# One diffusion trunk layer on one core: the output projection begun under the last two heads' normalisation, and the SwiGLU transposes moved behind the next group's first product

## The chip, the cores and the metric

The kernel runs on one core of one Trainium2 chip. The metric is device time in microseconds (us) of one execution. An execution under the profiler gives the trace that is read here; its own time stands beside the times of the runs without a profile.

## The reference

One layer of a trunk for 512 latent tokens (`x`, width 2048) and 256 context tokens, all float32. What is computed, in order:

```python
mod = silu(c) @ w_mod + b_mod                    # six rows of 2048: shift, scale, gate, twice
hx  = rms_norm(x, g_pre_mix) * (1 + mod[1]) + mod[0]
u, v, q, k, vv, g, df, db = split(hx @ w_in)     # 1024, 1024, 512, 512, 1024, 1024, 16, 16
a_x = gelu(u) * (w_s @ layer_norm(gelu(v)) + b_s)          # group A, 8 heads, chunks of 128
o   = bidirectional gated linear attention(q, k, vv, df, db; state of the context)   # group B, 4 heads of 256
gla = rms_norm(o per head) * out_g * silu(g)
y   = concat(a_x, gla) @ w_out                   # 2048 x 2048
x   = x + mod[2] * rms_norm(y, g_post_mix)
h2  = rms_norm(x, g_pre_ffn) * (1 + mod[4]) + mod[3]
f   = (silu(h2 @ w1) * (h2 @ w3)) @ w_ffn_out    # SwiGLU, 5632 hidden units
x   = x + mod[5] * rms_norm(f, g_post_ffn)
```

## The kernel before

Every product of two float32 matrices is done as three passes of a 32-bit reduced format (`three`, L298): each operand is split into a high part (a cast on ScalarE, ACT) and a low part (the difference, on VectorE, DVE), and TensorE (PE) multiplies high by high, low by high and high by low. Weights are streamed from HBM by DMAs that SyncE (SP) issues, 512 KB each, into a small ring of tiles, split, and used for 24 matmuls of 128x512. So each pair of contraction steps needs one landed load, one ACT cast of 128x1024, one DVE subtraction of 128x1024, in time.

**Stages around the change.** After the context tokens, four blocks of 512 columns are projected, `vv0`, `vv1`, `g0`, `g1` (PE tiles `vv0a` to `g1a`, 16 steps of 12 matmuls each). Under them the attention of the four heads runs as background work: scores by seven levels (`s`), transposed keys (`ktp`, copied to `ktok`), chunk states (`stp`, `st`), the outputs (`o`, copied to `kq`), the mean of their squares (`ms`), and a normalisation by ACT and DVE that ends in `kq` (L909 to L917). The silu of `g` (`ge`, L957) times `kq` (L965) is split into `yh`, `yl` (L942, `to_parts`): the contraction steps 8 to 15 of the output projection. Steps 0 to 7 come from group A (`reload_a`). Heads 0 and 1 give steps 8 to 11, heads 2 and 3 steps 12 to 15.

Then all background work is drained, the pools of the attention are closed, and the output projection runs in column blocks of 512: `wo0`, `wo1`, `wo2` over all four token tiles, `wo3` over two halves (`project`, L1026). Each block ends in squares for the norm and in a product with the gate row, `yo = y * gate[cg]`. The gate rows are themselves products of `c` with 2048 rows of `w_mod`: 16 loads of 512 KB (`m20w`, then `m21w`), each multiplied and added on DVE into `m20acc` or `m21acc` (L229), and one matmul with ones (`m20ps`, L265), two gate rows of 512 from each. The shift and scale of the second half of the layer are made the same way (`mf0` to `mf12`, with `fmodA`, `fmodB`).

The SwiGLU layer goes through the 5632 hidden units in 11 groups of 512. Each is a Strassen-like scheme of seven half-size products (`p1` to `p7`, tile `f3p` for group 3), whose weight tiles are named by letter (`f3a` to `f3e`, `f3z`, `f3y`), 48 matmuls each. At the end DVE and ACT form the units of 512 tokens (`f3u`, `f3g`), PE transposes them (16 transposes, `f3T`), ACT copies them (`f3t`) and writes them to a buffer in HBM (`g_dr`). The last stage reads that buffer back (`gr`, split into `gh`, `gl`) and multiplies with `w_ffn_out` (`fo`, 40 steps for each of four column blocks, in two chunks of 20; then `fz`). From group 3 on the last gate (`m50` to `m53`, 16 loads of 256 KB each) is made in the background.

**What sets the order.** The code is written out once; background work is a generator that a pump advances by `rate` steps after each contraction step of the foreground (`bg` for attention and transposes, `bgm` for products with `w_mod`). A scheduler then orders each engine's instructions; every engine executes its list in order. A few instructions are pinned to the place at which they were written (`keep_in_program_order`), `m20ps` and `mf12ps` among them. A load waits, on SP's list, until the buffer that it fills is free, and what stands behind it waits too. `load_behind` puts a load of `w_mod` after the weight load issued last.

**Buffers that the change touches.** `st2` holds the weight ring of the projection and the SwiGLU (tag `R`, 4 tiles of 128x1024) and, before, four wide tiles `X`; `fp` holds 29 tiles of 128x512 (`fslot`). `st2` takes the place of `stg`, the ring of the stages before. PSUM has 6 banks for products and 2 for background work.

Of the kernel before, what the change touches and what calls it, by code (L numbers as in the profile page):

```python
# [9 lines left out]
F32 = mybir.dt.float32  # L10
# [8 lines left out]
P = 128  # L19
# [72 lines left out]
def trunk_kernel(ctx, tc, cmat, cmask, x, c, ctxt, c_ctx, w_mod, b_mod, g_pre_mix, g_post_mix, g_pre_ffn,  # L92
# [19 lines left out]
    def slot(name, dt=F32, shape=(P, 512)):  # L112
        return s2.tile(list(shape), dt, tag="s2", bufs=NS, name=name)
# [94 lines left out]

    mod_bg = mod_pool(stg, 3, 1, load_behind)

    def mod_acc(c0, n, parts, cvec, name, tiles, pin=False):
# [42 lines left out]
    def mod_row(base, cb, grow, dst, name, tiles, keep=None, nb=2):  # L254

        n = f"{name}{cb}"
        for acc in mod_acc(base + cb * nb * 512, nb * 512, 1, cx, n, tiles):
            if acc is None:
                yield
        yield  # L260
        for j in range(nb):
            b = cb * nb + j
            gb = slot(n + f"g{j}")
            nc.scalar.dma_start(gb, grow[0:1, b * 512:(b + 1) * 512].to_broadcast([P, 512]))
            ps = bank(n + f"ps{j}", False)  # L265
# [503 lines left out]
    def exp_tables():  # L769
        tc.keep_in_program_order(S.preload_act_table_set("natural_log_exp_and_others"))  # L770
# [175 lines left out]
    def reload_a(k):  # L946
        if 6 <= k < 14:
            t = slot(f"ya{k - 6}")
            nc.sync.dma_start(t, a_dr[k - 6])
            to_parts(t, k - 6)  # L950

    for g in range(2):
        accs = block_ws(w_in[0], OG + g * 512, 4, f"g{g}", reload_a if g == 1 else None)
        evs = []
        for b, ps in enumerate(accs):
            ev = slot(f"ge{g}_{b}")
            S.activation(ev, ps, AF.Silu)  # L957
            evs.append(ev)
        if g == 0:
            exp_tables()  # L960
        while not (head_done[2 * g] and head_done[2 * g + 1]):
            bg.run(1)
        for b, ev in enumerate(evs):
            k = g * 4 + b
            V.tensor_tensor(out=ev, in0=ev, in1=kq[k // 2][:, k % 2, :], op=ALU.mult)  # L965
            to_parts(ev, 8 + k)
    bg.drain()
    bgm.drain()
    gl_ctx.close()
    pp_ctx.close()  # L970


    stg_ctx.close()
    fp = ctx.enter_context(tc.tile_pool(name="fp", bufs=1, reuse_waits="tile"))
    st2 = ctx.enter_context(tc.tile_pool(name="st2", bufs=1, side="right", reuse_waits="tile"))
    g_dr = dr.tile([HID // P, P, 512], F32, name="g_dr")
    gate2_dr = dr.tile([4, 512], F32, name="gate2_dr")

    def fslot(name, dt=F32):
        return fp.tile([P, 512], dt, tag="f", bufs=NF, name=name)  # L980

    def chain_tile(name):
        return st2.tile([P, 1024], F32, tag="X", bufs=4, name=name)

    def raw2(name):
        return st2.tile([P, 1024], F32, tag="R", bufs=4, name=name)
# [21 lines left out]
                pump()  # L1008

    mod_late = (chain_tile, chain_tile, load_behind)  # L1010
    gate = [slot(f"gm{b}") for b in range(4)]

    def mods_out():
        for b in range(2):
# [6 lines left out]
    bgm.add(mods_out())  # L1021
    bgm.rate = 1.5
    oss = cp.tile([P, NT, 4], F32, name="oss")
    yo = [[None] * 4 for _ in range(NT)]

    def project(cg, toks, name):  # L1026
        accs = [bank(f"{name}{t}") for t in toks]
        for k, wp in stream2(w_out[0], cg * 512, 0, KT, name):
            for i, t in enumerate(toks):
                three(accs[i], cut(yT[k], t * P, P), wp, k == 0, k == KT - 1)  # L1030
        for i, t in enumerate(toks):
            S.activation(junk, accs[i], AF.Square, accum_out=oss[:, t, cg:cg + 1])
            yo[t][cg] = fslot(f"yo{t}{cg}")
            V.tensor_tensor(out=yo[t][cg], in0=accs[i], in1=gate[cg], op=ALU.mult)

    def residual(t0):

# [109 lines left out]
    def ffn_top(gi, new):  # L1147

        n = f"f{gi}"
        raw = [None] * NQ  # L1150
        ps = two(n + "p1")
        for q in range(NQ):
            raw[q] = blk(gi, 0, 0, q, new(f"{n}X{q}"))
            product(1, q, ps, parts(raw[q], f"{n}a{q}"), NQ)
            pump()
        u = [fslot(f"{n}u{t}") for t in range(2)]
        for t in range(2):
            S.copy(u[t], ps[t])
        return u, raw

    def ffn_top2(gi, u):

        n = f"f{gi}"
        ps = two(n + "p2")
        for q in range(NQ):
            product(2, q, ps, parts(blk(gi, 1, 0, q, raw2(f"{n}b{q}")), f"{n}b{q}"), NQ)
            pump()
        a1 = [fslot(f"{n}g{t}") for t in range(2)]
        vtt(a1, ps, u, ALU.add)
        for t in range(2):  # L1170
            S.activation(a1[t], a1[t], AF.Silu)
        return a1

    early_u, early_a = [], []

    def ffn_group(gi):
        n = f"f{gi}"
# [23 lines left out]
        for q in range(NQ):  # L1201
# [21 lines left out]
        toks = a1 + u
        for f in range(4):
            ps = bank(f"{n}T{f}", False)
            for t in range(NT):
                T.transpose(ps[:, t * P:(t + 1) * P], toks[t][:, f * P:(f + 1) * P], ident)
            gt = slot(f"{n}t{f}")
            S.copy(gt, ps)
            nc.scalar.dma_start(g_dr[gi * 4 + f], gt)  # L1230
# [17 lines left out]
    def hidden(k0, nk):

        for k in range(k0, k0 + nk, 2):  # L1250
            r = raw2(f"gr{k}")
            nc.sync.dma_start(r.rearrange("p (k c) -> p k c", k=2), g_dr[k:k + 2].rearrange("k p c -> p k c"))
            for j in range(2):
                hi, lo = slot(f"gh{k + j}", F32R), slot(f"gl{k + j}", F32R)
                S.copy(hi, r[:, j * 512:(j + 1) * 512])  # L1255
                V.tensor_tensor(out=lo, in0=r[:, j * 512:(j + 1) * 512], in1=hi.bitcast(F32), op=ALU.subtract)  # L1256
                yield (hi, lo)

    LAST = 4
    wl_ = []  # L1260
# [90 lines left out]
```

## Time and profile before

| | |
|---|---|
| median of 3 runs | 2372.94 us (2368.51 to 2376.49) |
| the profiled execution | 2380.68 us, span of its instructions 2378.9 us |
| PE busy | 2274.8 us, 96% of the span |
| DVE, ACT busy | 1596.6 us (67%), 987.0 us (41%) |
| mean granted TensorE clock | 0.981 |
| chain that ended last | PE 66%, DVE 17%, DMA 12% |

A matmul of 128x512 is recorded with 389 ns, but the next starts 227 ns later: matmuls overlap, so busy time says little, and the count of matmuls in a stretch says what PE could do. Idle time of PE in the middle of a dense stage is time lost, unless another stage makes up for it.

### The profile page before, as it was taken

To read this page: it belongs to the slowest core of one execution; us is meant where nothing else is said; L and a number is where in the kernel's file an instruction comes from. 1 tells how busy PE (TensorE), PEld (TensorE's weight loads), DVE (VectorE), ACT (ScalarE), POOL (GpSimd) and SP (SyncE) were. 2 spreads that over 40 slices of the span, in tenths; PEclk is the share of its full clock that TensorE was granted. 3 is DMA by queue.
4 is the path that set the end of the run, shared out by engine and by line. 5 is a ranking of instruction groups with operands and counts; after the bars stand their busy time and mean duration, and the time that the engine had idled before them with its cause. 6 is when DMAs were issued, how large, how long until landed. Compare 5 with 4: busy or idle time off the path is not lost.

```text
span 2378.9 us, 27845 instructions
## 1 busy us (share of the span) xinstructions
PE 2274.8 (96%) x10386; PEld 1844.1 (78%) x10386; DVE 1596.6 (67%) x2072; ACT 987.0 (41%) x1509; POOL 15.5 (1%) x24
## 2 busy tenths in 40 slices
PE   7999999999996999989899999999999899999998
PEld 2778888788885788767788778887778788888886
DVE  3886577677777745698778878888888632242346
ACT  4443234455574224754343444444344332241232
POOL 0000000000000000000000000000000000000000
PEclk9999999999998999999999999999999999999999
DMA  9967787744434965757667757766676542253344
GB/s 323 338 198 252 244 284 265 242 133 127 139 107 152 312 244 169 229 167 241 203 186 256 227 186 228 248 203 226 203 252 214 187 161 98 98 176 107 105 138 157
DMA packets 252013, 477.30 MB, mean 201 GB/s; under 512 B 21163, under 2 KB 32643, under 8 KB 251877
## 3 DMA queue, kind: packets, MB, share of 16 engines
q1 hardware_dynamic: 241152, 457.78, 58.9%
q10 hardware_dynamic: 10724, 17.74, 2.1%
q8 instruction: 81, 1.33, 0.2%
q14 instruction: 56, 0.45, 0.1%
HBM read 451.33 MB, written 24.13 MB: 200 GB/s over the span
## 4 chain that ended last, share of the span: by engine, by line
PE 66%; DVE 17%; DMA 12%; issue 2%; ACT 2%; SPq 0%; ACTq 0%; DVEq 0%
PE fo L116 18%; PE wo L116 6%; PE f1p L116 3%; PE f4p L116 3%; PE f6p L116 3%; PE f2p L116 2%; PE g0a L116 2%; PE v0a L116 2%; PE u1a L116 2%; PE fz L116 2%; PE vv1a L116 2%; PE cv L116 2%; PE q L116 2%; PE k L116 2%; PE u L116 2%
## 5 line engine op out<-in xcount | busy, mean ns | idle before, releaser
L1256 DVE TENSOR_TENSOR gl<-gr,gh 128x512 fp32r<-128x512 f32 x44 | 28.4, 688 | 32.3 <-ACT gh L1255 32.3
L1255 ACT CAST gh<-gr 128x512 fp32r<-128x512 f32 x44 | 25.1, 618 | 42.1 <-DMA gr<-g_dr 30.8
L993 DVE TENSOR_TENSOR fo_2l<-fo_r,fo_2h 128x1024 fp32r<-128x1024 f32 x8 | 9.8, 1225 | 30.0 <-ACT fo_2h L992 30.0
L832 ACT ACTIVATE lv<-lv 128x1024 f32<-128x1024 f32 x20 | 21.0, 1055 | 19.6 <-DVE lv L831 19.5
L116 PE MATMUL vv0a<-vv_0h,hxh 128*128 128x512 f32 x64 | 28.0, 437 | 0.0
L993 DVE TENSOR_TENSOR fo_0l<-fo_r,fo_0h 128x1024 fp32r<-128x1024 f32 x8 | 9.8, 1224 | 26.3 <-ACT fo_0h L992 26.3
L993 DVE TENSOR_TENSOR fo_18l<-fo_r,fo_18h 128x1024 fp32r<-128x1024 f32 x8 | 9.8, 1226 | 26.2 <-ACT fo_18h L992 26.2
L116 PE MATMUL vv1a<-vv_0h,hxh 128*128 128x512 f32 x64 | 27.0, 422 | 0.0
L1315 ACT ACTIVATE junk<-fc 128x512 bf16<-128x512 f32 x16 | 10.1, 631 | 40.7 <-DVE fc L1314 40.6
L833 DVE TENSOR_TENSOR lv<-lv,kq 128x1024 f32<-128x1024 f32 x20 | 24.4, 1220 | 3.8 <-ACT lv L832 3.8
L116 PE MATMUL g0a<-hxh,g_0h 128*128 128x512 f32 x64 | 26.7, 417 | 0.0
L116 PE MATMUL g1a<-hxh,g_0h 128*128 128x512 f32 x64 | 26.4, 412 | 0.3 <-ACT g_0h L277 0.3
L229 DVE SCALAR_TENSOR_TENSOR m20acc<-m20w,cpair,m20acc 128x1024 f32<-128x1024 f32 x16 | 20.5, 1283 | 8.9 <-DMA m20w<-in_w_mod_dram 8.7
L116 PEld LDWEIGHTS s<-lv 128*128 128x128 f32 x192 | 24.9, 191 | 2.1 <-issue 0.5
L993 DVE TENSOR_TENSOR fo_16l<-fo_r,fo_16h 128x1024 fp32r<-128x1024 f32 x8 | 9.8, 1224 | 24.6 <-ACT fo_16h L992 24.6
L116 PE MATMUL v1a<-v_0h,hxh 128*128 128x512 f32 x64 | 26.3, 410 | 0.0
L116 PE MATMUL vv0a<-vv_0l,hxh 128*128 128x512 f32 x64 | 26.0, 407 | 0.0
L993 DVE TENSOR_TENSOR fo_14l<-fo_r,fo_14h 128x1024 fp32r<-128x1024 f32 x8 | 9.8, 1226 | 23.9 <-ACT fo_14h L992 23.9
L116 PE MATMUL v1a<-v_0l,hxh 128*128 128x512 f32 x64 | 25.9, 404 | 0.0
L116 PE MATMUL vv0a<-vv_0h,hxl 128*128 128x512 f32 x64 | 25.9, 404 | 0.0
L116 PE MATMUL g1a<-hxl,g_0h 128*128 128x512 f32 x64 | 25.8, 403 | 0.0
L116 PE MATMUL v1a<-v_0h,hxl 128*128 128x512 f32 x64 | 25.7, 401 | 0.0
(3876 smaller groups left out, 7949.6 us busy)
## 6 DMA issues: line engine op xcount, KB each, us to landing
fo_r<-in_w_ffn_out_dram SPq DMA_DIRECT2D x80, 512.0 KB
gr<-g_dr SPq DMA_DIRECT2D x22, 512.0 KB
mx4w<-in_w_mod_dram SPq DMA_DIRECT2D x16, 512.0 KB
mx8w<-in_w_mod_dram SPq DMA_DIRECT2D x16, 512.0 KB
mx12w<-in_w_mod_dram SPq DMA_DIRECT2D x16, 512.0 KB
mc4w<-in_w_mod_dram SPq DMA_DIRECT2D x16, 512.0 KB
mc8w<-in_w_mod_dram SPq DMA_DIRECT2D x16, 512.0 KB
mc12w<-in_w_mod_dram SPq DMA_DIRECT2D x16, 512.0 KB
```

The source lines that it names most:

```text
L116: return T.matmul(o, lhsT=l, rhs=r, start=start, stop=stop)
L229: ins = V.scalar_tensor_tensor(out=acc, in0=raw[:, j].rearrange("p i c -> p (i c)"), scalar=cvec[:, k0 + j:k0 + j + 1], in1=acc, op0=ALU.m ...
L832: S.activation(lv, lv, AF.Exp)
L833: V.tensor_tensor(out=lv, in0=lv, in1=kq[h], op=ALU.mult)
L993: V.tensor_tensor(out=wl, in0=src, in1=wh.bitcast(F32), op=ALU.subtract)
L1255: S.copy(hi, r[:, j * 512:(j + 1) * 512])
L1256: V.tensor_tensor(out=lo, in0=r[:, j * 512:(j + 1) * 512], in1=hi.bitcast(F32), op=ALU.subtract)
L1315: S.activation(junk, f, AF.Square, accum_out=fss[:, cg:cg + 1])
```

## The change

The attention's last step (the product with `ge` for heads 2 and 3, and the closing of its pools) moves into the first column block of the output projection, ahead of its contraction step 12 (`attention_end`). Block 0 keeps its result without the gate, and is multiplied with `gate[0]` after block 1. The gate rows are begun at step 12 too; the weight ring is opened before. For that the background rate of `mf*` under `vv` and `g` rises from 0.6 to 0.85, so that it is drained before the projection. The transposes of a group's units are issued after the next group's first product (`turn_hidden`); those of the last group after four steps of the last stage, whose first eight `gh`, `gl` are read back inside group 10. `m50` to `m53` load tiles of 128x512 from `fslot`, one row block at a time, no longer pairs in the weight ring; their rate rises from 0.2 to 0.33 with 16 smaller steps in place of 8. The four wide tiles `X` move from `st2` to `fp`.

```diff
-        per = 1024 // w
+        per = width // w                    # mod_row passes width=nb * 512
...
-    bg.rate, bgm.rate = 2.4, 0.6
+    bg.rate, bgm.rate = 2.4, 0.85
...
+    def gated(g, evs):
+        while not (head_done[2 * g] and head_done[2 * g + 1]):
+            bg.run(1)
+        for b, ev in enumerate(evs):
+            k = g * 4 + b
+            V.tensor_tensor(out=ev, in0=ev, in1=kq[k // 2][:, k % 2, :], op=ALU.mult)
+            to_parts(ev, 8 + k)
...
+        exp_tables()
+        gates.append(evs)
         if g == 0:
-            exp_tables()
-        while not (head_done[2 * g] and head_done[2 * g + 1]):
...
+            gated(0, evs)
-    bg.drain()
     bgm.drain()
-    gl_ctx.close()
-    pp_ctx.close()
     stg_ctx.close()
...
     def chain_tile(name):
-        return st2.tile([P, 1024], F32, tag="X", bufs=4, name=name)
+        return fp.tile([P, 1024], F32, tag="X", bufs=4, name=name)
...
-            yield from mod_row(5 * D, b, g_post_ffn, None, "m5", (raw2, fslot, load_behind), gate2_dr, 1)
+            yield from mod_row(5 * D, b, g_post_ffn, None, "m5", (fslot, fslot, load_behind), gate2_dr, 1)
...
         for k, wp in stream2(w_out[0], cg * 512, 0, KT, name):
+            if before:
+                before(k)
...
+            if before:
+                S.copy(yo[t][cg], accs[i])
+            else:
+                V.tensor_tensor(out=yo[t][cg], in0=accs[i], in1=gate[cg], op=ALU.mult)
+
+    def attention_end(k):
+        nonlocal fp
+        if k == 12:
+            gated(1, gates[1])
+            bg.drain()
+            gl_ctx.close()
+            pp_ctx.close()
+            fp = ctx.enter_context(tc.tile_pool(name="fp", bufs=1, reuse_waits="tile"))
+            bgm.add(mods_out())
+            bgm.rate = 1.5
+            bgm.run(1)
...
-    exp_tables()
-    for cg in range(3):
-        project(cg, range(NT), f"wo{cg}")
+    project(0, range(NT), "wo0", attention_end)
+    project(1, range(NT), "wo1")
+    for t in range(NT):
+        V.tensor_tensor(out=yo[t][0], in0=yo[t][0], in1=gate[0], op=ALU.mult)
+    project(2, range(NT), "wo2")
...
+        if gi == HID // 512 - 1:            # in the last group, after its fifth product
+            for _ in range(8):
+                gT.append(next(src))
...
+        behind.append((gi, a1 + u))
+    def turn_hidden():                      # called after p1, p2 and p5 of a group, and at step 4 of fo
+        while behind:
+            gi, toks = behind.pop()         # the 16 transposes, 4 copies and 4 writes as before
...
-    bgm.rate = 0.2
+    bgm.rate = 0.33
```

The first place is PE's list from the end of `g1a` into `wo0`. `ktp`, `stp`, `o` and `ms` belong to head 3, `wo00h` to the first weight tile of block 0. Before:

```order
L871 MATMUL ktp_1_6389<-mats,kk_6334 128x128 x3
L116 MATMUL stp_1_0_6395<-vv_1_4038,ktok_1_6393 128x256
...
L116 MATMUL o_1_6422<-qt_6404,sini 128x128
L116 MATMUL ms_6438<-sq_6436,mats 128x512 x2
L116 MATMUL mf12ps<-mats,mf12acc 128x1 x8
L116 MATMUL wo_6534<-wo00h,yh_6002 128x512
```

And in the changed kernel:

```order
L871 MATMUL ktp_1_6478<-mats,kk_6387 128x128 x3
L116 MATMUL wo_6438<-wo00h,yh_6049 128x512
...
L116 MATMUL stp_1_0_6484<-vv_1_4038,ktok_1_6482 128x256
...
L116 MATMUL stp_1_1_6487<-vv_1_4036,ktok_1_6482 128x256
L116 MATMUL wo_6438<-wo02h,yh_6126 128x512
...
L116 MATMUL o_1_6541<-qt_6511,sini 128x128
L116 MATMUL wo_6438<-wo04h,yh_6220 128x512
...
L116 MATMUL ms_6557<-sq_6555,mats 128x512 x2
```

48 matmuls of `wo0` now stand between `ktp` and `o`, eight more ahead of `ms`, and 88 between `ms` and step 12, the first that needs heads 2 and 3. `mf12ps` stands ahead of the end of `g1a`.

The second place is SP's list from the last loads of the attention's stage on. `mf12w`, `m20w` are rows of `w_mod`, `wo0r` the projection's weights, `ya` group A's result. Before, and then in the changed kernel:

```order
L203 DMA mf12w_6500<-in_w_mod_dram 128x2x512
L203 DMA mf12w_6503<-in_w_mod_dram 128x2x512
L195 DMA wo0r_6538<-in_w_out_dram 128x2x512
L203 DMA m20w_6559<-in_w_mod_dram 128x1024
L203 DMA m20w_6574<-in_w_mod_dram 128x1024
L203 DMA m20w_6577<-in_w_mod_dram 128x1024
L195 DMA wo0r_6580<-in_w_out_dram 128x2x512
```

```order
L949 DMA ya_6297<-a_dr 128x512
L949 DMA ya_6337<-a_dr 128x512
L195 DMA wo0r_6442<-in_w_out_dram 128x2x512
L195 DMA wo0r_6490<-in_w_out_dram 128x2x512
...
L195 DMA wo1r_6857<-in_w_out_dram 128x2x512
L203 DMA m20w_6727<-in_w_mod_dram 128x1024
L203 DMA m20w_6742<-in_w_mod_dram 128x1024
```

All eight loads of `wo0` and the first two of `wo1` now stand ahead of the first load for the gates.

The third place is PE's list at the end of group 10 (`f10p` its last product, `fo` the last stage, `m53ps` the last gate's matmul). Before, and then in the changed kernel:

```order
L116 MATMUL f10p_14701<-f10y3h,S7l_8512 128x512
L1227 MATMUL f10T_14864<-mats,f10g_14437 128x128
...
L1227 MATMUL f10T_14888<-mats,f10u_14355 128x128
L116 MATMUL m53ps_14898<-m53acc,mats 128x512
L116 MATMUL fo_14902<-fo_0h,gh_14914 128x512
```

```order
L116 MATMUL f10p_14753<-f10y3h,S7l_8516 128x512
L116 MATMUL m53ps_14942<-m53acc,mats 128x512
L116 MATMUL fo_14946<-fo_0h,gh_14714 128x512
...
L116 MATMUL fo_14949<-fo_2h,gl_14729 128x512
L1276 MATMUL f10T_15016<-mats,f10g_14452 128x128
```

48 matmuls of `fo` stand ahead of the transposes. On SP seven of the sixteen `m53w` loads now stand between the last load of group 10 and the first of `fo`, where before none did, and four `gr` loads stand ahead of the last eight weight loads of group 10 (`f10z`, `f10y`).

## Rows read from the trace of the kernel before

**Rows 1.** Windows of 10 us at the projection's start: us, busy time (instructions), clock, DMA, GB/s.
```profile
762.00:772.00 10.00, 2.22 (x7) 1.86 (x8) 5.41 (x10) 3.55 (x4) 0.95 (x1) 0.50 0.51 174
772.00:782.00 10.00, 8.87 (x32) 6.68 (x31) 8.23 (x8) 1.04 (x1) 0.00 (x0) 0.75 0.97 344
```

**Rows 2.** Waits of PE, 700 to 840 us: total, times, longest.
```profile
PE mf12ps L116 <- issue: 7.9, 1, 7.9
PE wo L116 <- ACT wo00h L992: 7.8, 1, 7.8
PE stp L116 <- ACT ktok L873: 2.4, 2, 1.8
PE ms L116 <- ACT sq L903: 1.8, 1, 1.8
```

**Rows 3.** Waits of SP's queue, 700 to 780 us.
```profile
SPq L195 <- DVE kq L917: 12.9, 1, 12.9
```

**Rows 4.** Timeline of PE: start us, us, what (two places).
```profile
732.25 0.49 PE L871 MATMUL ktp<-mats,kk 128*128 128x128 f32 x3
...
826.64 0.39 PE L116 MATMUL wo<-wo10h,yh 128*128 128x512 f32 x1
```

**Rows 5.** Chain that ended last, PE's pieces: start us, us, what.
```profile
695.76 0.43 PE stp L116 x2
...
702.53 2.68 PE o L116 x24
...
714.94 1.72 PE ms L116 x4
...
814.16 0.86 PE m20ps L116 x2
...
1890.28 435.49 PE fo L116 x1920
```

**Rows 6.** Timeline of ACT, 737 to 770 us.
```profile
737.79 0.48 ACT L873 COPY ktok<-ktp 128x384 f32<-128x384 f32 x1 [0.36 <-PE ktp L871]
...
754.02 1.28 ACT L911 ACT_TABLE_LOAD   x1
...
765.67 0.62 ACT L942 CAST yh<-ge 128x512 fp32r<-128x512 f32 x1 [9.07 <-DVE ge L965]
...
769.47 1.04 ACT L992 CAST wo00h<-wo0r 128x1024 fp32r<-128x1024 f32 x1 [1.28 <-DMA wo0r<-in_w_out_dram]
```

**Rows 7.** Gate tiles: ns min/median/max of one, first and last start us.
```profile
L229 DVE SCALAR_TENSOR_TENSOR m20acc<-m20w,cpair,m20acc x16: 1278/1284/1286, 771.3 to 805.4; 128x1024 f32<-128x1024 f32 x16
...
L229 DVE SCALAR_TENSOR_TENSOR m21acc<-m21w,cpair,m21acc x16: 1274/1283/1289, 809.1 to 848.2; 128x1024 f32<-128x1024 f32 x16
```

**Rows 8.** Window of the gates' loads, columns as in rows 1.
```profile
770.00:850.00 80.00, 74.68 (x299) 58.09 (x300) 60.28 (x52) 16.81 (x22) 0.96 (x1) 0.94 0.91 309
```

**Rows 9.** Window of the stages vv0 to g1.
```profile
465.00:732.00 267.00, 265.98 (x1426) 225.41 (x1425) 203.32 (x338) 155.49 (x323) 1.91 (x2) 0.99 0.40 129
```

**Rows 10.** Waits of PE in the SwiGLU groups, 1080 to 1860 us.
```profile
PE f2p L116 <- DVE f2c0l L993: 5.7, 1, 5.7
PE f0T L1227 <- DVE f0g L1141: 1.9, 1, 1.9
PE f5p L116 <- ACT f5d0h L992: 1.3, 1, 1.3
...
PE f4T L1227 <- ACT f4t L1229: 0.2, 1, 0.2
PE f6p L116 <- DVE f6a2l L993: 0.2, 1, 0.2
```

**Rows 11.** Timeline of DVE and PE at the end of group 10.
```profile
1855.64 1.30 DVE L1141 TENSOR_TENSOR f10u<-f10p,f10u 128x512 f32<-128x512 f32 x2
...
1877.36 0.39 PE L116 MATMUL f10p<-f10y3h,S7l 128*128 128x512 f32 x1
```

**Rows 12.** Wait of PE, 1860 to 1900 us.
```profile
PE f10T L1227 <- DVE f10g L1141: 5.5, 1, 5.5
```

More of the change, by code (lines that the diff above doesn't have):

```diff
@@ L209, in trunk_kernel, with mod_acc @@
     mod_bg = mod_pool(stg, 3, 1, load_behind)
-    def mod_acc(c0, n, parts, cvec, name, tiles, pin=False):
+    def mod_acc(c0, n, parts, cvec, name, tiles, pin=False, width=1024):
         w = parts * n
@@ L256, in mod_row @@
         n = f"{name}{cb}"
-        for acc in mod_acc(base + cb * nb * 512, nb * 512, 1, cx, n, tiles):
+        for acc in mod_acc(base + cb * nb * 512, nb * 512, 1, cx, n, tiles, width=nb * 512):
             if acc is None:
@@ L950, in reload_a @@
             to_parts(t, k - 6)
+    def gated(g, evs):
[5 more added lines that the diff above has]
+            to_parts(ev, 8 + k)
+    gates = []
     for g in range(2):
@@ L958, in trunk_kernel @@
             evs.append(ev)
+        exp_tables()
+        gates.append(evs)
         if g == 0:
-            exp_tables()
-        while not (head_done[2 * g] and head_done[2 * g + 1]):
[L962 to L966, printed above, removed]
-    bg.drain()
+            gated(0, evs)
     bgm.drain()
-    gl_ctx.close()
-    pp_ctx.close()
     stg_ctx.close()
-    fp = ctx.enter_context(tc.tile_pool(name="fp", bufs=1, reuse_waits="tile"))
     st2 = ctx.enter_context(tc.tile_pool(name="st2", bufs=1, side="right", reuse_waits="tile"))
@@ L1010, in trunk_kernel @@
     mod_late = (chain_tile, chain_tile, load_behind)
-    gate = [slot(f"gm{b}") for b in range(4)]
+    gate = [None] * 4
     def mods_out():
+        for b in range(4):
+            gate[b] = slot(f"gm{b}")
         for b in range(2):
@@ L1018, in gate_ffn, with project @@
         for b in range(4):
-            yield from mod_row(5 * D, b, g_post_ffn, None, "m5", (raw2, fslot, load_behind), gate2_dr, 1)
-    bgm.add(mods_out())
-    bgm.rate = 1.5
+            yield from mod_row(5 * D, b, g_post_ffn, None, "m5", (fslot, fslot, load_behind), gate2_dr, 1)
     oss = cp.tile([P, NT, 4], F32, name="oss")
     yo = [[None] * 4 for _ in range(NT)]
-    def project(cg, toks, name):
+    def project(cg, toks, name, before=None):
         accs = [bank(f"{name}{t}") for t in toks]
         for k, wp in stream2(w_out[0], cg * 512, 0, KT, name):
+            if before:
+                before(k)
             for i, t in enumerate(toks):
@@ L1033, in project @@
             yo[t][cg] = fslot(f"yo{t}{cg}")
-            V.tensor_tensor(out=yo[t][cg], in0=accs[i], in1=gate[cg], op=ALU.mult)
+            if before:
[13 more added lines that the diff above has]
+            bgm.run(1)
     def residual(t0):
@@ L1158, in ffn_top @@
             S.copy(u[t], ps[t])
+        turn_hidden()
         return u, raw
@@ L1171, in ffn_top2, with hidden @@
             S.activation(a1[t], a1[t], AF.Silu)
+        turn_hidden()
         return a1
+    def hidden(k0, nk):
+        for k in range(k0, k0 + nk, 2):
+            r = raw2(f"gr{k}")
+            nc.sync.dma_start(r.rearrange("p (k c) -> p k c", k=2), g_dr[k:k + 2].rearrange("k p c -> p k c"))
+            for j in range(2):
+                hi, lo = slot(f"gh{k + j}", F32R), slot(f"gl{k + j}", F32R)
+                S.copy(hi, r[:, j * 512:(j + 1) * 512])
+                V.tensor_tensor(out=lo, in0=r[:, j * 512:(j + 1) * 512], in1=hi.bitcast(F32), op=ALU.subtract)
+                yield (hi, lo)
     early_u, early_a = [], []
+    gT, src = [], hidden(0, 20)
     def ffn_group(gi):
@@ L1190, in ffn_group @@
             pump()
+        turn_hidden()
         p6 = two(n + "p6")
@@ L1222, in ffn_group @@
         vtt(u, u, p7, ALU.mult)
[L1223 to L1230, printed above, removed]
+        behind.append((gi, a1 + u))
+    behind = []
+    def turn_hidden():
+        while behind:
+            gi, toks = behind.pop()
+            n = f"f{gi}"
+            for f in range(4):
+                ps = bank(f"{n}T{f}", False)
+                for t in range(NT):
+                    T.transpose(ps[:, t * P:(t + 1) * P], toks[t][:, f * P:(f + 1) * P], ident)
+                gt = slot(f"{n}t{f}")
+                S.copy(gt, ps)
+                nc.scalar.dma_start(g_dr[gi * 4 + f], gt)
     bg.rate = 1.0
@@ L1246, in trunk_kernel @@
     facc = [[None] * 4 for _ in range(NT)]
[L1248 to L1257, printed above, removed]
     LAST = 4
@@ L1276, in trunk_kernel @@
     for ci, (k1, nk) in enumerate(((0, 20), (20, 20))):
-        gT = []
-        src = hidden(k1, nk)
+        if ci:
+            gT, src = [], hidden(k1, nk)
         for cg in range(4):
@@ L1284, in trunk_kernel @@
             for k, wp in stream2(w_ffn_out[0], cg * 512, k1, nk, f"fo{ci}{cg}_"):
-                if cg == 0:
+                if len(gT) <= k:
                     gT.append(next(src))
+                if k == 4:
+                    turn_hidden()
                 for t in range(NT):
```

1 line of the change is left out of this document (added).

## The prediction

> **What bounds the kernel now.** I read the windows of the span first: PE is busy 96% of it, so time can only be won where PE stands or runs at the lower clock. Then the chain that ended last: its largest piece is `fo`, 1920 matmuls in 435.49 us, or 0.2268 us for each [rows 5]. That is PE's pace with nothing missing, and I count every stretch against it. The stretch that falls short most lies between the projections and the output projection. In the timeline head 3's `ktp` begins at 732.25 and the first matmul of `wo1` at 826.64 [rows 4]: 94.4 us. The work in it is 192 matmuls of `wo0` (43.5), two heads' `o` (2 x 2.68), `ms` (1.7), six `stp` at half of 0.43 (1.3) [rows 5], six `ktp` at a third of 0.49 (1.0) [rows 4], 16 `mf12ps` at a twenty-fourth of 2.68 each (1.8) and two pairs of `m20ps` (2 x 0.86) [rows 5]: 56.4 us. So 38.0 us are lost there. The waits of PE name half of it: 7.9 ahead of `mf12ps`, 7.8 on `wo00h`, 2.4 on `ktok`, 1.8 on `ms` [rows 2]. The rest is a low clock, 0.50 and then 0.75 of full speed in the two windows where `wo0` starts [rows 1], dependent single matmuls of `stp`, and weights of `wo0` that come late. The last follows from SP's queue: the first load of `wo0` stood 12.9 us behind `kq` [rows 3], and when it went out, the gates' loads stood between those of `wo0`, with the DMA engines busy 0.97 of the time [rows 1].
>
> In the SwiGLU groups PE waits little: five waits at transposes, from 1.9 to 0.2 (3.8 together), and nine for weights from group 3 on, from 1.3 to 0.2 (6.9 together), beside one of 5.7 at `f2c0l` [rows 10]. At the end of group 10 it waits 5.5 ahead of the transposes [rows 12]. The last product begins its last matmul at 1877.36 [rows 11], `fo` starts at 1890.28 [rows 5]: 12.9 us.
>
> **The change part by part.**
>
> *The attention's end.* PE gets 48 matmuls of `wo0` (10.9 us) between `ktp` and `o`, eight more ahead of `ms`, and 88 (20.0 us) between `ms` and step 12. The normalisation that these 88 cover ran in the trace from `kq`'s squares to the cast of `yh`, with two ACT table loads of 1.28 in it [rows 6]. The wait of 7.9 was one for the mean and the last `mf12acc`; `mf12` is now done earlier, and 20 us cover the normalisation. What is left is the front: ACT has two evictions of `ge`, then `ktok` 0.48, a table load 1.28, `yh` 0.62 and `wo00h` 1.04 [rows 6] before the first matmul of `wo0`, some of it under `ktp` and `stp`. I take 4 us for that, and 2 us for `o`, `ms` and single late casts: 6 lost in place of 38.0, a gain of 32. If the 20 us didn't hide the normalisation and the clock stayed low, only the two waits at the front that loads caused (7.8) would go; if PE ran without a hole, 36. Bounds 8 and 36.
>
> *Transposes behind the next product.* The 16 transposes are work all the same; what goes are the waits of 3.8 [rows 10]. PE's list was interleaved before too: the transposes stood among the next group's matmuls, only earlier. I take 3, bounds 0 and 3.8.
>
> *`m5` out of the weight ring.* With it goes a competitor for the ring's four tiles from group 3 on, the cause I see for the nine waits of 6.9 in all [rows 10]. But the smaller loads wait for a free tile of `fslot`, and while one waits, the weight loads behind it on SP's list wait too. Of the 29 tiles I count 16 for the two sums, 6 for `u`, `g` and the products, 4 held units and one accumulator, so two stay free. I take half, 3.5; bounds -3 (the waits grow by half) and 6.9. The wait of 5.7 at `f2c0l` stands before `m5` begins and stays.
>
> *From group 10 into `fo`.* Of the 12.9 us, 16 transposes at 2.68/24 (1.8) and one `m53ps` (0.9, as `m20ps`) remain work [rows 5], so 10 can be won. Against it: four `gr` loads now stand ahead of the `f10z`, `f10y` weights on SP's list. Where `f10u`'s end at 1855.64 [rows 11] comes ahead of the split of `f10z` on DVE, as it now stands, I cost about 4 us at `p5`; and the third and fourth bank of `fo` come free behind the same chain of DVE, 1 us. I take 5; bounds 0 and 10.
>
> *`mf12` drained earlier.* Some 12 additions of 1.28 (as the like gate rows, [rows 7]) move under `vv0` to `g1`, where DVE is busy 203.32 of 267 us [rows 9]: 219 of 267, 0.82 of the time. PE has 0.99 of full clock there and no room, so each late weight counts. I take a cost of 2; bounds 0 and 5.
>
> *The gates.* `m20ps` and `m21ps` are pinned in PE's list, at step 8 of `wo1` and step 4 of `wo2`. The gates' first load now stands behind ten loads of `wo`. With four ring tiles and 24 matmuls (5.44 us) for each load it can go out about 31 us after the end of `g1a`. Before, the additions took from 771.3 to 849.5 [rows 7], 78 us; with 6 for the first load to land, the second gate is ready 115 us after `g1a`. PE arrives at `m21ps` after 432 matmuls (98.0), the other work (some 11) and the front of 4: at 113. I take a cost of 2; bounds 0 and 11 (first load two ring tiles later, 2 x 5.44). `m20ps` has about 7 us of slack by the same count. While `m21ps` waits, the rest of `wo2` is queued behind it.
>
> The gain is 32 + 3 + 3.5 + 5 - 2 - 2 = 39.5 us. The profiled execution took 2380.7 (its span 2378.9 and 1.8 around it), which gives 2341. It lies 7.7 us above the median of the runs, 2372.9; taken from that, 39.5 gives 2333.
>
> **Rivals.** *B: half is given back at the gates.* Over the 80 us of the gates' loads the DMA engines were busy 0.91 of the time, moving 309 GB/s [rows 8]. 16 MB and a bit more of gate rows must still pass, now under PE at full pace, which draws `wo`'s weights faster. Then `m21ps` waits the 11, weights come some 5 later, and the 5 of the end are not won: a gain of 39.5 - 9 - 5 - 5 = 20, 2353. For it: the share; against: the loads begin some 30 us earlier relative to the matmuls that need them. [...]
>
> *C: all terms at their better ends*: 35 + 4 + 7 + 10 and no costs, 56, hence 2317. For it: PE's lists have no other hole; against: six terms must all hold.
>
> *E: the change doesn't do what it says*: the loads of `wo0` wait after all for a tile that the attention holds, as the 12.9 of [rows 3], and PE still stands until the normalisation is over. Only the 8 of the lower bound remain: 2365. Against it: SP's list has `wo0`'s loads right behind `ya`.
>
> *D, slower: SP's list blocks at `m5`'s tiles.* 64 loads of 256 KB need an `fslot` tile each with two free. If one is not free until the units of a group are written out, SP holds the weights behind it. From 0.62 us for each (39.5 / 64) the gain is gone, and at 1.28, the duration of one addition that a load would wait for [rows 7], the time is 2333 + 82 = 2415. For it: only two tiles to spare. Against it: an addition frees a tile at once, and eight loads fall on a group, which lasts some 71 us (780 us of [rows 10] in 11 groups).
>
> **How the numbers follow.** Forecast 2333, chance 0.62; B 0.15, C 0.12, E 0.06, D 0.05. The forecast's own terms with errors of half their bounds give 2322 to 2343. For eight in ten I take in C's half and B: 2314 to 2356. A measurement of this kernel can tell about 0.3%, 7 us, from no change. Faster by more: the forecast, B, C and most of E, less what I don't see, 0.90; within it 0.05 (the rest of E, D at small price); slower 0.05 (D).
>
> **What would show it.** Right: PE's waits on `wo00h` and ahead of `mf12ps` are gone; the clock is at 1.0 of full from `g1` into `wo1`; the first matmul of `wo1` comes about 62 us after head 3's `ktp`; the wait ahead of `f10T` is gone and `fo` begins right behind `f10p` and `m53ps`. The price shows as waits at `m20ps`, `m21ps` (step of the gates), at `f10z` (step of the end), and in SP's queue at `m5w`. Wrong it is if PE stands at step 12 of `wo0` (the normalisation not covered), if `m21ps` waits over 11, or if the waits for weights in groups 3 to 10 exceed 10 together.

## The result and the profile after

The changed kernel took 2347.27 us (median of four runs, 2346.42 to 2349.05), where the kernel before took 2372.8: a ratio of 0.9894 (95% interval 0.9876 to 0.9912), 25.5 us less. Run again beside the experiments it took 2345.56, ratio 0.9875 (0.9861 to 0.9888), 29.6 us less. The forecast was 2333. The direction was right and the time is inside the range, but a quarter to a third of the gain that was forecast (39.5) did not come, and the parts came out differently from their terms.

| | before | after |
|---|---|---|
| profiled execution, span | 2380.68, 2378.9 us | 2349.05, 2347.2 us |
| PE busy | 2274.8 us (96%) | 2262.3 us (96%) |
| DVE, ACT busy | 1596.6, 987.0 us | 1593.5, 982.2 us |
| mean granted clock | 0.981 | 0.990 |
| chain that ended last | PE 66%, DVE 17%, DMA 12% | PE 64%, DMA 15%, DVE 15% |

Where the time went is read from the starts of the first matmuls of each stage, by which a trace is cut into stretches; the last one ends at the start of the last matmul. All the kernels run here are in one table (us, one execution in each row; the time ahead of `vv0` also varies, by up to 9 us, before anything changed is reached, and is left out):

| kernel | vv0 to g0 | g1, attention, wo0 | wo1, wo2 | wo3 | groups 0-2 | groups 3-9 | group 10 to end |
|---|---|---|---|---|---|---|---|
| before | 211.8 | 163.5 | 89.0 | 49.0 | 269.6 | 563.9 | 570.7 |
| before2 (again) | 209.0 | 158.3 | 89.6 | 48.1 | 267.4 | 563.4 | 570.3 |
| after | 213.7 | 130.0 | 102.2 | 49.0 | 261.8 | 563.7 | 567.2 |
| after2 (again) | 212.2 | 127.7 | 102.2 | 48.1 | 263.8 | 563.5 | 566.7 |
| att | 211.8 | 127.7 | 102.5 | 48.0 | 269.1 | 570.8 | 572.8 |
| turn | 210.1 | 159.7 | 89.9 | 48.9 | 261.0 | 563.5 | 566.0 |
| m5 | 210.5 | 161.7 | 88.8 | 48.6 | 268.0 | 566.7 | 572.4 |
| nom5 | 212.9 | 127.7 | 100.8 | 48.7 | 262.3 | 563.6 | 567.0 |
| nopre | 213.4 | 129.7 | 101.6 | 48.6 | 263.2 | 564.0 | 565.9 |
| late | 213.2 | 127.6 | 101.2 | 48.1 | 262.0 | 566.3 | 574.0 |
| slow | 212.3 | 127.1 | 102.7 | 48.3 | 262.7 | 564.1 | 568.1 |
| evict | 214.4 | 127.3 | 92.9 | 48.6 | 263.0 | 564.2 | 566.6 |
| pre4 | 211.8 | 128.1 | 92.9 | 48.2 | 264.7 | 564.0 | 562.8 |
| comb | 214.2 | 127.6 | 93.8 | 48.2 | 265.2 | 565.2 | 566.2 |

By the means of the two executions of each kernel the stretches change by +2.6, -32.0, +12.9, 0, -5.7, 0 and -3.6, together -25.8: the difference that the runs show. The single execution that the prediction was made from stood 11.5 us above the second one over these stretches, 5.2 of it at the attention, so it was a long example of its kernel, and the comparison of the first two traces (31.6 us) overstates the gain.

The hole is closed. PE's timeline, as in [rows 4], shows head 3's `ktp`, the first matmul of `wo0` and that of `wo1` (start us, us, what):

```profile
737.20 0.49 PE L871 MATMUL ktp<-mats,kk 128*128 128x128 f32 x3
...
741.30 0.96 PE L116 MATMUL wo<-wo00h,yh 128*128 128x512 f32 x3 [0.47 <-ACT wo00h L995]
...
793.73 0.39 PE L116 MATMUL wo<-wo10h,yh 128*128 128x512 f32 x1
```

From `ktp` to `wo1` 56.5 us pass where it was 94.4. Of the work counted there, `mf12ps` (1.8) and `m20ps` (1.7) have moved out, so 52.9 are work and 3.6 are lost, in place of 38.0. In the second execution of each kernel it is 56.5 in place of 89.2. The windows of 10 us, columns as in [rows 1], show the granted clock that goes with it: the first two lie at `wo0`'s start and stand at full speed, the third, in `wo2`, at 0.74. The last is the like of [rows 8]:

```profile
741.00:751.00 10.00, 9.70 (x43) 7.92 (x43) 6.62 (x8) 4.09 (x6) 0.00 (x0) 1.00 0.53 183
751.00:761.00 10.00, 10.00 (x69) 8.93 (x67) 1.71 (x2) 3.28 (x4) 0.00 (x0) 1.00 0.30 104
...
842.70:852.70 10.00, 3.25 (x9) 2.35 (x8) 8.36 (x10) 0.76 (x1) 0.00 (x0) 0.74 0.93 318
790.00:870.00 80.00, 71.38 (x296) 56.50 (x295) 55.05 (x51) 19.41 (x32) 0.96 (x1) 0.96 0.85 287
```

PE's waits from 690 to 870 us, in place of [rows 2] (waits of 7.9, 7.8, 2.4 and 1.8), have a new line at their head (the four longest):

```profile
PE wo L116 <- DVE yo L1042: 6.7, 1, 6.7
PE wo L116 <- DVE wo114l L996: 1.5, 1, 1.5
PE stp L116 <- ACT ktok L873: 0.7, 1, 0.7
PE wo L116 <- ACT wo00h L995: 0.5, 1, 0.5
```

L1042 is the eviction of a finished accumulator with its gate row, here of `wo1`'s. It frees a PSUM bank: of the six banks `wo1` holds four, so the third accumulator of `wo2` waits for it. PE's timeline has the place:

```profile
842.63 0.39 PE L116 MATMUL wo<-wo20h,yl 128*128 128x512 f32 x1
849.77 0.79 PE L116 MATMUL wo<-wo20h,yh 128*128 128x512 f32 x1 [6.75 <-DVE yo L1042]
850.36 0.63 PE L116 MATMUL wo<-wo20l,yh 128*128 128x512 f32 x1
...
854.48 0.39 PE L116 MATMUL wo<-wo20h,yl 128*128 128x512 f32 x1
```

`wo1`'s last matmul began at 841.27, and its gate row had been written by 828.3. What held the eviction is DVE's own list, in its timeline (in brackets the idle time before, and what ended it):

```profile
842.49 1.28 DVE L229 SCALAR_TENSOR_TENSOR m21acc<-m21w,cpair,m21acc 128x1024 f32<-128x1024 f32 x1 [0.33 <-DVE m21acc L229]
845.32 1.28 DVE L229 SCALAR_TENSOR_TENSOR m21acc<-m21w,cpair,m21acc 128x1024 f32<-128x1024 f32 x1 [1.55 <-DMA m21w<-in_w_mod_dram]
846.52 1.22 DVE L996 TENSOR_TENSOR wo22l<-wo2r,wo22h 128x1024 fp32r<-128x1024 f32 x1
847.83 1.28 DVE L229 SCALAR_TENSOR_TENSOR m21acc<-m21w,cpair,m21acc 128x1024 f32<-128x1024 f32 x1
849.03 2.47 DVE L1042 TENSOR_TENSOR yo<-wo,gm 128x512 f32<-128x512 f32 x4
```

The evictions stand behind additions for the other gate, which wait for their loads, and these take 5.6 us each while the DMA engines are 0.93 busy. The chain that ended last has one of these loads as a piece of its own; the addition at 845.32 follows it:

```profile
839.63 5.60 DMA m21w<-in_w_mod_dram
```

After the stop the matmuls follow each other 0.43 us apart from 850.36 to 854.20, then 0.23 again: 2 us more. The granted clock is 0.50 from 850 to 854 and 1.00 from 854.4 to 860. The Trainium skill (TensorE: Matmul & The Clock Gate, "Wait — 56ns, not 53.3ns?") gives 426.7 ns between matmuls of 512 columns at 1.2 GHz and 215.7 at 2.4; the trace agrees with the first, and shows 226.8 for the second [rows 5], which is what the sums here use.

### The profile page after: what moved, and what is told of

Read it like the earlier page. It is cut to its first block, busy times and chain, and to the rows that moved or that the text cites. A ratio compares the mean times of both kernels' runs of the same rounds, so it can differ in the third digit from the quotient of the medians.

```text
span 2347.2 us, 27855 instructions
## 1 busy us (share of the span) xinstructions
PE 2262.3 (96%) x10386; PEld 1836.9 (78%) x10386; DVE 1593.5 (68%) x2072; ACT 982.2 (42%) x1509; POOL 15.5 (1%) x24
## 4 chain that ended last, share of the span: by engine, by line
PE 64%; DMA 15%; DVE 15%; issue 3%; ACT 2%; SPq 0%; DVEq 0%; ACTq 0%
PE fo L116 19%; PE wo L116 4%; PE f1p L116 3%; PE f9p L116 3%; PE f2p L116 3%; PE vv1a L116 2%; PE u1a L116 2%; PE fz L116 2%; PE cv L116 2%; PE g1a L116 2%; PE f7p L116 2%; PE q L116 2%; PE vv0a L116 2%; PE u L116 2%; PE g0a L116 2%
## 5 line engine op out<-in xcount | busy, mean ns | idle before, releaser
L229 DVE SCALAR_TENSOR_TENSOR m20acc<-m20w,cpair,m20acc 128x1024 f32<-128x1024 f32 x16 | 20.5, 1284 | 12.6 <-DMA m20w<-in_w_mod_dram 12.4
L996 DVE TENSOR_TENSOR fo_8l<-fo_r,fo_8h 128x1024 fp32r<-128x1024 f32 x8 | 9.8, 1226 | 26.2 <-ACT fo_8h L995 26.2
L996 DVE TENSOR_TENSOR fo_0l<-fo_r,fo_0h 128x1024 fp32r<-128x1024 f32 x8 | 9.8, 1223 | 25.5 <-ACT fo_0h L995 25.5
L996 DVE TENSOR_TENSOR fo_10l<-fo_r,fo_10h 128x1024 fp32r<-128x1024 f32 x8 | 9.8, 1224 | 24.1 <-ACT fo_10h L995 24.1
L229 DVE SCALAR_TENSOR_TENSOR m21acc<-m21w,cpair,m21acc 128x1024 f32<-128x1024 f32 x16 | 20.5, 1282 | 7.9 <-DMA m21w<-in_w_mod_dram 7.3
L996 DVE TENSOR_TENSOR fo_12l<-fo_r,fo_12h 128x1024 fp32r<-128x1024 f32 x8 | 9.8, 1226 | 23.5 <-ACT fo_12h L995 23.5
L116 PE MATMUL g0a<-hxh,g_0l 128*128 128x512 f32 x64 | 25.7, 402 | 0.0
```

What stands on the lines that cost most here:

```text
L116: return T.matmul(o, lhsT=l, rhs=r, start=start, stop=stop)
L996: V.tensor_tensor(out=wl, in0=src, in1=wh.bitcast(F32), op=ALU.subtract)
```

## The experiments

Each kernel ran beside the kernel before, and ratios are to that kernel, so that kernels of different series are compared by ratio or by the stretches above.

**One part at a time: att, turn, m5, and the kernel before once more.** The whole diff is split in three; the wide tiles `X` in the other pool and the rate of 0.85 belong to att.

```diff
 # att = changed kernel with these undone:
-        turn_hidden()          # after p1, p2, p5, and at step 4 of fo
+        turn_hidden()          # at the end of its own group
-                gT.append(next(src))   # eight, inside group 10
-  "m5", (fslot, fslot, load_behind) ... bgm.rate = 0.33
+  "m5", (raw2, fslot, load_behind) ... bgm.rate = 0.2
 # turn = kernel before, with only the first two of these changes
 # m5   = kernel before, with only the third
```

> The attention part alone on the kernel before: projection begun early, its first block kept without the gate, X tiles in the other pool, rate 0.85 under vv and g; transposes, m5 and the reading back of group 10 as before. Theory (the two traces: start of wo3 19.7 us earlier, of which 13 were lost again at the gates): about 20 us of the change's 25.5 are this part, ratio 0.992 (2353), with the same wait of about 7 us for the evictions of wo1. Rival (terms of the prediction): 32 - 2 - 2 = 28 us, 0.988, and the other parts lose a little.

> The transposes behind the next product and the reading back inside group 10 alone on the kernel before; attention and m5 as before. Theory (traces): nothing in groups 3 to 9, 4 us at the f2c0l wait and in groups 0 to 2, 3 to 6 at the end: 5 to 9 us, ratio 0.997. Rival (the prediction's terms): 3 + 5 = 8 us, half of it in groups 3 to 9. Second rival: the wait at f2c0l stays 5.7 and only the end is won: 4 us, 0.998.

> m5's loads alone as 128x512 tiles of fslot at rate 0.33, on the kernel before. Prediction's term: waits for weights in groups 3 to 10 fall from 6.9 to about half, 3.5 us, ratio 0.9985. Rival (trace of the changed kernel: as many waits, at other places): 0 within 2 us, 1.000. Seven m53w loads then stand ahead of fo's: if these delay fo, slower by 1 to 4 us.

> The kernel before, unchanged, profiled once more: whether the 7.7 us by which its profile lay above its median belong to one execution. If so its time is within 4 us of 2373, and the waits of 7.9 and 7.8 us ahead of mf12ps and wo0 are the same while others are shorter. Rival: profiling always costs this kernel 7 us, 2380.

Measured: att 2364.63 us, ratio 0.9957 (0.9941 to 0.9974), 10 us faster; turn 2363.01, 0.9950 (0.9931 to 0.9969), 12 us faster; m5 2378.88, 1.0016 (1.0000 to 1.0032), no gain and up to 8 us lost; before2 2367.35 in its one execution. So profiling does not cost this kernel 7 us; two executions of one kernel differ by that much. The waits of 7.9 and 7.8 were there again (6.8 and 7.9).

att fell short of both of its expectations and turn went beyond its own. m5 gained nothing, as its rivals had it, and not the 3.5 of the prediction. In the table the transposes' part gains 7.5 us in groups 0 to 2 and 4.5 behind group 9, nothing between; the first is the wait at `f2c0l`, which the prediction had left standing. DVE's timeline of the kernel before, and then of the changed one, shows why it went:

```profile
1165.97 2.36 DVE L1188 TENSOR_TENSOR f2X<-f2X,f2c 128x1024 f32<-128x1024 f32 x2
1169.20 1.23 DVE L1188 TENSOR_TENSOR f2X<-f2X,f2c 128x1024 f32<-128x1024 f32 x1 [0.88 <-DMA f2c<-in_w_ffn_in_dram]
1174.01 1.23 DVE L1188 TENSOR_TENSOR f2X<-f2X,f2c 128x1024 f32<-128x1024 f32 x1 [3.58 <-DMA f2c<-in_w_ffn_in_dram]
1175.15 1.28 DVE L1141 TENSOR_TENSOR f2g<-f2p,f2u 128x512 f32<-128x512 f32 x2
1176.35 1.22 DVE L993 TENSOR_TENSOR f2c0l<-f2X,f2c0h 128x1024 fp32r<-128x1024 f32 x1
```

```profile
1145.03 2.35 DVE L1225 TENSOR_TENSOR f2X<-f2X,f2c 128x1024 f32<-128x1024 f32 x2
1150.00 1.23 DVE L1225 TENSOR_TENSOR f2X<-f2X,f2c 128x1024 f32<-128x1024 f32 x1 [2.63 <-DMA f2c<-in_w_ffn_in_dram]
1151.15 1.22 DVE L996 TENSOR_TENSOR f2c0l<-f2X,f2c0h 128x1024 fp32r<-128x1024 f32 x1
```

The split that PE needs, `f2c0l`, depends on the first of four additions. Before, it stood in DVE's list behind all four and two products, and the last addition waited 3.58 us for its load. With the transposes moved the scheduler puts it behind three. Both att (wait 5.5) and m5 (5.2) keep the old order, turn and the whole change (1.9, 1.8) have the new one: the part is shown, though it is the order on DVE that changed and not a wait of the transposes.

att won 33 us at the attention (its stretch against the mean of 160.9), lost 13 in `wo1` and `wo2`, and then 7 more in groups 3 to 9, where it changes no line, only the pool of the wide tiles `X`. Its longest waits from there to the end of group 10, beside `f10T`'s, stand at places where the kernel before has none:

```profile
PE f7p L116 <- DVE f7e0l L996: 2.7, 1, 2.7
PE f7T L1271 <- DVE f7g L1164: 2.4, 1, 2.4
PE f9p L116 <- DVE f9c1l L996: 1.8, 1, 1.8
PE f10p L116 <- DVE f10c1l L996: 1.5, 1, 1.5
```

On DVE's list `f7e0l` stands there behind the group's additions of `f7u` and `f7w`, before it stood ahead of them. The three ratios multiplied give 0.9923, the whole 0.9875 to 0.9894, so 7 to 11 us of the whole's gain belong to no part alone. By the table they lie in groups 3 to 9, where att loses 7.1, m5 3.0 and the whole nothing.

**The wait at `wo2`: evict and slow.** There are two theories of the 13 us. The prediction's step said that `m21ps` stands too early in PE's list. The trace says that the evictions stand too late in DVE's.

```diff
 # evict                                        # slow
-            if before:                          yield from mod_row(2 * D, b, ...)
+            if cg < 2:                         +bgm.rate = 1.0
                 S.copy(yo[t][cg], accs[i])
 ...
     project(2, range(NT), "wo2")
+    for t in range(NT):
+        V.tensor_tensor(out=yo[t][1], in0=yo[t][1], in1=gate[1], op=ALU.mult)
```

> The changed kernel, but wo1's four accumulators are copied out by ACT as wo0's are, and multiplied with gate[1] after wo2; loads, rates and pins unchanged. Theory: the 6.9 us at wo2's third bank come from DVE's list, where the evictions stand behind gate additions that wait for their loads; without it PE does not stop, the clock does not fall (2 us more), and m21ps finds its sum nearly done: 6 to 9 us faster than the changed kernel, 2339. Rival (the prediction's step): the data of m21 are what is late, and the wait moves to m21ps or to wo2's weights: 0 to 3 us, 2345 to 2347.

> The changed kernel with the rate of the gates' background work 1.0 in place of 1.5 from the second gate row pair on: on PE's list m21ps moves from step 4 of wo2 to step 10, while SP's and DVE's lists keep the loads and additions where they are. The prediction priced the gates by m21ps standing too early: then the loss in wo2 falls by 7 or more. Theory now: the stop is at the evictions of wo1 behind the additions on DVE, so the wait of about 7 stays and wo2 lasts the same 54 us.

Measured: evict 2343.24 us, ratio 0.9847 (0.9829 to 0.9865); `wo1` and `wo2` take 92.9 us in place of 102.2. (By ratio alone evict and after2, below, still touch: 0.9865 and 0.9861.) All that PE waits for from 780 to 900 us is this:

```profile
PE wo L116 <- DVE wo114l L996: 0.5, 1, 0.5
PE wo L116 <- DVE wo14l L996: 0.2, 1, 0.2
PE wo L116 <- DVE wo22l L996: 0.2, 1, 0.2
```

The additions still wait for their loads, as this one of DVE's timeline:

```profile
848.16 1.28 DVE L229 SCALAR_TENSOR_TENSOR m21acc<-m21w,cpair,m21acc 128x1024 f32<-128x1024 f32 x1 [1.85 <-DMA m21w<-in_w_mod_dram]
```

`m21ps` stands where it stood on PE, and PE does not wait at it. In slow (2344.13 in one execution) `m21ps` came 39 us after `wo2`'s first matmul in place of 20, and the wait did not go, it grew to

```profile
PE wo L116 <- DVE yo L1043: 8.7, 1, 8.7
```

with 102.7 us for `wo1` and `wo2`. So the place of `m21ps` was not the cause, and the evictions' place on DVE was. What remains in evict over the kernel before, 92.9 against 89.3, is `m20ps` (1.7, moved here) and some 2 us of small gaps.

**m5 taken back: nom5.**

```diff
-  "m5", (fslot, fslot, load_behind) ... bgm.rate = 0.33
+  "m5", (raw2, fslot, load_behind) ... bgm.rate = 0.2
```

> The changed kernel with m5's loads back in the weight ring at rate 0.2: attention and transposes only. Theory A (the parts add): m5 alone cost 4 us on the kernel before, so without it 2343. Theory B (m5's loads matter only with the new timing: the attention part alone lost about 7 us in groups 7 to 9 with the ring shared): 2350 to 2354. Theory C (which waits the order of the groups happens to have): within 2 us of 2347.

Measured: 2345.25 us, ratio 0.9855 (0.9836 to 0.9874), against 0.9894 and 0.9875 with m5 moved. Groups 3 to 9 take 563.6, as with it (563.7, 563.5) and before (563.9, 563.4). Theory B of this expectation falls: with the transposes moved too, the ring shared with `m5` costs nothing there. Between A and C the intervals don't decide; that the move gains nothing by itself is shown by the run m5, whose interval begins at 1.0000. nom5 has `X` in the same pool as att and differs from it in the transposes and the reading back alone, and loses nothing there, so the pool alone does not cost att its 7 us.

**The reading back in group 10: nopre, late, pre4.** The changed kernel waits in group 10 and starts `fo` without a gap. Its waits from 1060 to 1900 us, in place of [rows 10, 12], and PE's timeline at `fo`'s start, in place of [rows 11]:

```profile
PE f10p L116 <- ACT f10z0h L995: 2.3, 1, 2.3
PE f2p L116 <- DVE f2c0l L996: 1.8, 1, 1.8
PE f10p L116 <- DVE f10y0l L996: 1.7, 1, 1.7
PE f5p L116 <- DVE f5c3l L996: 1.2, 1, 1.2
...
PE f1T L1276 <- ACT f1t L1278: 0.2, 1, 0.2
```

```profile
1855.92 0.40 PE L116 MATMUL f10p<-f10y3h,S7l 128*128 128x512 f32 x1
1856.16 1.02 PE L116 MATMUL m53ps<-m53acc,mats 128*128 128x512 f32 x2
1856.62 0.80 PE L116 MATMUL fo<-fo_0h,gh 128*128 128x512 f32 x1
```

```diff
         vtt(u, p4, u, ALU.add)
-        if gi == HID // 512 - 1:
-            for _ in range(8):                 # nopre: none at all
-                gT.append(next(src))           # pre4 (on evict): range(4)
 ...
             product(7, q, p7, parts(y, f"{n}y{q}"), NQ)
+            if gi == HID // 512 - 1 and q >= 2:     # late
+                for _ in range(4):
+                    gT.append(next(src))
```

> The changed kernel without the eight gh, gl read back inside group 10; fo reads them back itself as before. Theory (prediction's cost of 4 us at p5, trace 2.5 at f10z0 and 1.9 at f10y0): group 10 is 4 to 6 us shorter; fo then waits for its first gl behind DVE's chain of group 10, and if that costs as much as before (about 5) the time is the same, 2347. Rival: fo's first gl comes before the chain and nothing is lost: 2342.

> The changed kernel with the eight gh, gl read back four at the third and four at the fourth step of group 10's last loop, so that two gr loads stand behind two pairs of f10z, f10y on SP's list and the rest behind three. Theory: the waits at f10z0 and f10y0 (4.4) go and fo still starts without a wait: 4 to 5 us faster than the changed kernel, 2342. Rival: the waits move to f10z3 and f10y3, 2346 to 2347.

> The changed kernel with wo1 copied out by ACT (as in the run evict) and four gh, gl read back inside group 10 in place of eight. Theory: evict's 8 us, and group 10 and fo's first block together 2 to 4 us shorter than with eight (f10z0's split now stands ahead of half of the gl on DVE): 10 to 12 us faster than the changed kernel. Rival: the same 6 us are lost wherever the reading back stands, since f10's chain on DVE must end before the third bank of fo is free: 8 us, as evict.

Measured: nopre 2350.53 us, ratio 0.9884 (0.9865 to 0.9903), the same as the changed kernel; late 2356.18, 0.9907 (0.9890 to 0.9923), slower than after2's 0.9875, though the interval of the first series reaches into it; pre4 2336.5, 0.9843 (0.9823 to 0.9862). PE's longest waits from 1740 to 1900 us show where the time goes in nopre, then late, then pre4:

```profile
PE fo L116 <- ACT gh L1206: 2.1, 1, 2.1
PE fo L116 <- DVE f10w L1164: 1.3, 1, 1.3
```

```profile
PE fo L116 <- ACT fo_0h L995: 5.8, 1, 5.8
PE fo L116 <- DVE fo_0l L996: 1.7, 1, 1.7
```

```profile
PE f10p L116 <- DVE f10b2l L996: 0.6, 1, 0.6
PE f10p L116 <- DVE f10y2l L996: 0.5, 1, 0.5
PE fo L116 <- DVE f10w L1166: 0.3, 1, 0.3
```

What the reading back saves `fo` it takes from group 10, so eight gain nothing (567.0 with them, 565.9 without). Late only pushes `fo`'s own weights back. With four, in pre4, `f10z0l` stands on DVE ahead of half of the `gl`, and neither side waits long: the last stretch takes 562.8, in evict, with eight, 566.6. That is one execution of each, and the ratios don't show it: pre4 has 0.9843, evict 0.9847.

**What beats both: after2, comb.** comb is pre4 with m5 back in the ring.

```diff
 # pre4, and
-  "m5", (fslot, fslot, load_behind) ... bgm.rate = 0.33
+  "m5", (raw2, fslot, load_behind) ... bgm.rate = 0.2
```

> The changed kernel, unchanged, on the same chip as the next ones, so that these are compared with it and not with times of another chip. Theory: ratio to the kernel before as in the result, 0.989; the wait of about 7 us at wo2's third bank and those at f10z0 and f10y0 are there again. Rival: the ratio depends on the chip and comes out under 0.986, as the two variants that were faster.

> As pre4, and m5's loads back in the weight ring at rate 0.2. Theory: m5's move is worth nothing within 2 us, so the time is that of pre4; no m53w load then stands ahead of fo's loads, which may give 1 to 2 us. Rival: m5's move costs 4 us or more (as on the kernel before), and this is the fastest, 4 to 9 us ahead of pre4.

Measured in one series: after2 2345.56 us, ratio 0.9875 (0.9861 to 0.9888), comb 2335.0, 0.9829 (0.9816 to 0.9843), pre4 0.9843. comb is 0.5% ahead of the changed kernel, its interval clear of that of after2; pre4 overlaps by a hair. comb and pre4 can't be told apart: by their intervals m5's place in the ring is worth between 9 us won and 2 lost. Nor does comb repeat pre4's last stretch. It takes 566.2 in comb's trace, which is the slowest of its five executions (2341.76), and PE waits in group 10 again, at another place:

```profile
PE f10p L116 <- DVE f10y1l L996: 2.1, 1, 2.1
```

So a gain of four read back over eight is not shown; what both share with evict is `wo1` and `wo2` in 93 to 94 us.

## Why the prediction was right in sign and too large

The steps as the prediction put them, with the mean of two traces of each kernel:

- **The attention's end, 32: 31.8.** From `ktp` to `wo1` 91.8 us became 56.5, of which 3.5 is work that moved out (forecast: about 62, with that work still counted). The waits on `wo00h` and ahead of `mf12ps` went (0.5 is left), the clock stayed at full, nothing waits at step 12. But the normalisation was not only covered, it also became shorter: from `kq`'s squares to the cast of `yh` it took 17.4 us (748.24 to 765.67 [rows 6]) and now takes 10.5 (759.93 to 770.41). `mf12`'s additions no longer stand in it on DVE, and neither do the two table loads on ACT (752.08 and 754.02, [rows 6]); one at 738.38 stands ahead of it. The last `yl` is written at 772.4 and step 12 begins at 782.9, so the old length would have fitted too. Rival E did not happen: the eight loads of `wo0` went out from 709 to 750 us, all ahead of the normalisation.
- **`mf12` drained earlier, cost 2: 4.0.** From `vv0` to `ktp` 279.5 us became 285.3, of which 1.8 is the work of `mf12ps`. The price did not show as late weights, as the prediction had it, but in the attention's scores, which wait 2.2 and 1.5 us for DVE (`lv`, L828).
- **The gates, cost 2, bounds 0 and 11: 11.2.** This is the step that failed: 12.9 less the 1.7 of `m20ps`, just over the upper bound. The prediction asked only when the *data* of the gates come (and 115 us against 113 was not far off: `m21acc`'s last addition began at 853.8, 117 us after `g1`'s last matmul). It read the additions as a supply to `m21ps`, and did not ask what stands behind them on DVE, though it said of `m21ps` what is queued behind that on PE. Before, the last addition began 24 us ahead of `wo1`'s end (848.2 [rows 7]), now it begins 12 us behind it. `wo0`'s evictions stood among additions before too, but the two right ahead of them had their data, and PE lost 0 and 0.5 us there. evict shows that the evictions' place alone is 9 us of it, slow that `m21ps` is none. Rival B had the gates as the place and the DMA load as the reason (0.85 of the time busy, [rows 8] 0.91), and the time it gave, 2353, lies nearer to 2347 than the forecast does; but its waiting instruction was wrong, and with the same loads evict has no such wait.
- **Transposes, 3: 5.7, most of it at another place.** The waits of `f0T`, `f1T`, `f4T`, `f5T` and `f10T` shrank or went, and groups 3 to 9 gained nothing, since as many small waits for `b2l` and `y2l` came. The 5.7 lie in groups 0 to 2: the wait at `f2c0l`, which the sum held to be none of the change's, fell from 5.7 and 5.3 to 1.8 and 1.5 us, and the matmuls behind it ran at a granted clock of 0.50 before (1177.6 to 1182.0) and run at 1.00 now (1152.4 to 1157.0). The prediction had no step for this, so that these us came is luck.
- **`m5`, 3.5, bounds -3 and 6.9: 0, and -4 alone.** Nine waits for weights of 6.9 were put down to the ring's competitor. With it gone groups 3 to 9 take as long as before, and the waits for weights there grew from 6.7 to 8.0; so the competitor was not what set them. That the order on DVE sets them is likely by their places and not shown. One of the prediction's own signs of being wrong came with it: over 10 of such waits in groups 3 to 10 together, where 12.4 were measured, 4.5 of them in group 10. SP's list did not block: rival D did not happen. (A group lasts 80.6 us, 563.9 / 7, and not the 71 of that rival, which makes it only less likely.)
- **The end, 5: 3.6.** The 12.9 us before `fo` became 0.7 (12.2 won), group 10 grew by 6.2 (cost named: 4) and `fo` by 2.4 (transposes 1.8 and 0.6).

Together 31.8 - 4.0 - 11.2 + 5.7 + 0 + 3.6 = 25.9. The range held the time because the gates' upper bound was in it, by way of rival B, and because `f2c0l` gave back what `m5` did not.

Open: why the scheduler writes group 7's splits behind the group's additions in att and not in nom5 was not tried; no run changes only that order, and none moves only the pool of `X`, so the cause of att's 7 us is argued from its waits and not shown.

## What to carry to other kernels

When a stage is pulled forward over background work, list for each in-order engine what comes to stand *behind* the background's instructions, not only who needs their result: an addition that waits for a load stops the eviction behind it, and that holds a PSUM bank, and that stops TensorE. Put what frees a bank on the engine with no such queue (here ACT). And take a term from a second execution before pricing waits of a few us: two profiles of one kernel differed by 11.5.

## What the runs showed that was not expected

A wait can shrink by a change that was not aimed at it, because the scheduler writes the order anew: the wait at `f2c0l` lost 3.8 us by the transposes' move, and att lost 7 in groups whose code it leaves alone. Parts measured alone did not add up: 10 + 12 - 4 is 18 us, the whole 25 to 30.
